# Down product of a gated MLP: sums of activations before each chain of products, the b chain continued from a1, and the plain units moved forward

## The chip, the cores and the metric

One Trainium2 chip, one of its cores. The metric is the device time of one execution in microseconds, as the median of several runs.

## What is computed

The kernel computes one layer of a decoder trunk on 512 tokens of 1024 channels in float32: three token mixers behind one input projection, their merge, and a gated MLP. The part around the change is the MLP, with D_FF = 3072:

```python
h = rms_norm(x, norm_ffn)
up = causal_dwconv(h @ w_up, ffn_conv_w, ffn_conv_b)      # 512 x 6144
a, b = up[..., :3072], up[..., 3072:]
x = x + (gelu(a) * b) @ w_down                            # 3072 -> 1024
out = rms_norm(x, final_norm)
```

## The kernel before

**Products.** Every float32 product is made of three products on TensorE: each operand is split into a high part (`split` L97, a copy on ScalarE that rounds) and a low part (L98, a subtraction on VectorE), and `mm3` (L104) adds high times high, high times low and low times high into one bank of PSUM. A product can start when the split of its operands is done.

**Up product.** The 3072 channels are 24 tiles of 128. A plain up unit makes one half of a tile (half 0 goes through the gelu, half 1 is the factor): 24 products, then the evacuation `up_evac` with the convolution (a scaled copy on ScalarE L1169, two scalar_tensor_tensor on VectorE L1171). With its second half a tile is finished by `up_mix`: the gelu on ScalarE L1183, the product on VectorE L1184. Tiles 0 to 19 are kept as float32 (`whole`); tiles 20 to 23 are split at once into a high and a low part (`halves`), which only the last stage of the kernel reads (`down_units`).

**Down product.** The first 20 tiles go through a scheme of seven products of half-size blocks instead of eight (`down_fast`, built by `seven`, L282 on). It has five groups p (four tiles each) and seven keys, a1, a2, c1, c2, b1, b2, b3; one key of one group is a fast unit of 12 products of 128x512. All five groups of one key follow each other and add up in the same two banks of PSUM; a2 goes on in a1's banks, c2 in c1's, b2 and b3 in b1's. After the last group of a key its two banks are read (`read`): VectorE adds them into the residual (`put`, L1335). a1's result is needed in several places; two copies on ScalarE (L1341) keep it, and three puts for each bank follow. Which activations a key multiplies: a1, a2 and b3 take quarters of the tiles as they are, c1, c2, b1 and b2 take sums of them. `sums(p)` makes six tensor_tensors of 128x256 for a group (L1311 to L1313), `sum4(p)` two more (L1321). `act_ready` then splits the quarter or sum. The weights of a1, c1, b1 and b3 stand in one buffer for each group, B11, into which GpSimd's accumulating transfers (`add`, L299) add the next matrix; those of b2 in B12 in the same manner; B21 and B22 are loaded directly.

**What sets the order.** Each unit carries steps with a lead: a step with lead 3 is issued three units ahead of the unit's products. `us` holds the seven plain units left at that point, u0 to u6: the second half of tile 20, then both halves of tiles 21, 22 and 23. `blend(us, down_fast(...))` puts five fast units behind each of them: u0 and a1, u1 and a2, u2 and c1, u3 and c2, u4 and b1, u5 and b2, u6 and b3. A planner turns this program into one stream for each engine; an engine runs its stream in order and stands still at the first instruction whose inputs, or whose buffer, are not ready. Buffers for activations, their splits, loaded weights and the evacuated halves all come from one pool `apool` of 51 slots; the splits of weights have four buffers each.

Of the kernel before, what the change touches and what calls it, by code (L numbers as in the profile page):

```python
# [13 lines left out]
AF = mybir.ActivationFunctionType  # L14
ALU = mybir.AluOpType
# [3 lines left out]
P = 128  # L19
# [20 lines left out]
AHEAD = 2  # L40
BRANCHES = (2, 0, 1)
NRAW = 3
HT = S // 2
# [14 lines left out]
def trunk(ctx: ExitStack, tc: tile.TileContext, x, xT, mem, memT, par, wdecay, wch, wv, wg, wmk,  # L58
          wmv, wrg, wbr, wout, wup, wdown, wdown2, gffn, gfin, out):
    nc = tc.nc  # L60
# [11 lines left out]
    def nm(s):  # L72
        uid[0] += 1
        return f"{s}_{uid[0]}"

    def fslot(shape=(P, S)):
        return apool.tile(list(shape), F32, tag="s", name=nm("f"))
# [7 lines left out]
    def bank(shape=(P, S)):  # L85
        return psm.tile(list(shape), F32, tag="mm", name=nm("mm"))

    def sbank(shape=(P, S)):
        return pss.tile(list(shape), F32, tag="sm", name=nm("sm"))
# [5 lines left out]
    def split(hi, lo, src, eng=None):  # L95

        nc.scalar.activation(hi, src, AF.Copy)  # L97
        return (eng or nc.vector).tensor_tensor(out=lo, in0=src, in1=hi.bitcast(F32), op=ALU.subtract)  # L98
# [45 lines left out]
    def made_unit(pre, fn):  # L144

        prog.append(("unit", pre, fn))
# [62 lines left out]
    ps = sbank((P, P))  # L209
# [72 lines left out]

    def seven(src, n, np, lhs, pre, read, far=AHEAD):

        raw, w, banks = {}, {}, {}

        def load(q, p):
            raw[q, p] = [fslot((P, n)) for _ in range(2)]
            for j in range(2):
                loads.append(nc.sync.dma_start(raw[q, p][j], src(q, p)[:, j, :]))

        def add(to, q, p):

            for j in range(2):
                nc.gpsimd.dma_start(raw[to, p][j], src(q, p)[:, j, :], accum_op=ALU.add)  # L299

        def direct(q, p):
            raw[q, p] = wpool.tile([P, 2, n], F32, tag="raw", name=nm("raw"), bufs=NRAW)
            loads.append(nc.sync.dma_start(raw[q, p], src(q, p)))

        def ready(key, q, p):
            hi = wpool.tile([P, 2, n], F32R, tag="whi", name=nm("whi"))
            lo = wpool.tile([P, 2, n], F32R, tag="wlo", name=nm("wlo"))
            if isinstance(raw[q, p], list):
                for j in range(2):
                    split(hi[:, j, :], lo[:, j, :], raw[q, p][j])  # L310
            else:
                split(hi, lo, raw.pop((q, p)))
            w[key, p] = hi, lo

        def run(key, p):
            ws = w.pop((key, p))
            b = key[0]
            for i in range(2):
                if key[1] == "1" and p == 0:
                    banks[b, i] = bank((P, n))  # L320
                mm3(banks[b, i], [(*lhs(key, p, j, i), ws[0][:, j, :], ws[1][:, j, :]) for j in range(2)],
                    key[1] == "1" and p == 0, p == np - 1, key[1] != "1")
                if p == np - 1:
                    read(key, i, banks[b, i])

        steps = {
            "a1": ("B11", [(6, lambda p: load("B11", p))]),
            "a2": ("B21", [(far, lambda p: direct("B21", p))]),
            "c1": ("B11", [(6, lambda p: add("B11", "B12", p))]),
            "c2": ("B22", [(far, lambda p: direct("B22", p))]),  # L330
            "b1": ("B11", [(6, lambda p: add("B11", "B22", p))]),
            "b2": ("B12", [(10, lambda p: load("B12", p)), (7, lambda p: add("B12", "B22", p))]),
            "b3": ("B11", [(6, lambda p: add("B11", "B21", p))]),
        }
        us = []
        for key, (q, before) in steps.items():
            for p in range(np):
                us.append(([(m, lambda f=f, p=p: f(p)) for m, f in before] +
                           [(AHEAD, lambda key=key, q=q, p=p: ready(key, q, p))] +
                           [(m, lambda f=f, p=p: f(p)) for m, f in pre.get(key, ())],  # L340
                           lambda key=key, p=p: run(key, p)))
        return us

    def run(*parts):

        for p in parts:
            if isinstance(p, tuple):
                unit(*p)
            else:
                for v in p:  # L350
                    made_unit(*v) if isinstance(v, tuple) else step(v)

    def blend(us, fast, steps=()):

        for i, u in enumerate(us):
            unit(*u)
            for l, f in ((fast, lambda v: made_unit(*v)), (steps, step)):
                for v in l[len(l) * i // len(us):len(l) * (i + 1) // len(us)]:
                    f(v)
# [407 lines left out]
    b2 = [u for d in range(KD) for u in branch(2, oc, d)]  # L767
# [173 lines left out]
    at = lambda a, i: by_chunk(a)[:, :, i:i + 1].broadcast_to([DK, NT, P])  # L941
# [350 lines left out]

    kept = {}

    def down_fast(at, np, acts, first, last):

        a_in, a_sp = {}, {}

        def sums(p):

            A = {}
            for j in range(2):
                ev, od = acts(2 * (2 * p + j)), acts(2 * (2 * p + j) + 1)
                for r in range(2):
                    A[1 + r, 1, j], A[1 + r, 2, j] = ev[:, r * HT:(r + 1) * HT], od[:, r * HT:(r + 1) * HT]
            s1, s2 = fslot((P, 2, HT)), fslot((P, 2, HT))
            tt = nc.vector.tensor_tensor
            for j in range(2):  # L1310
                tt(out=s1[:, j, :], in0=A[2, 1, j], in1=A[2, 2, j], op=ALU.subtract)  # L1311
                tt(out=s2[:, j, :], in0=s1[:, j, :], in1=A[1, 1, j], op=ALU.subtract)
                tt(out=A[2, 1, j], in0=A[1, 1, j], in1=A[2, 1, j], op=ALU.subtract)  # L1313
            both = lambda r, c: [A[r, c, j] for j in range(2)]
            a_in.update({("a1", p): both(1, 1), ("a2", p): both(1, 2), ("c1", p): s1, ("b1", p): s2,
                         ("b2", p): both(2, 1), ("b3", p): both(2, 2)})

        def sum4(p):
            a_in["c2", p] = a_in["a1", p]
            for j in range(2):  # L1320
                nc.vector.tensor_tensor(out=a_in["a1", p][j], in0=a_in["a2", p][j], in1=a_in["b1", p][:, j, :],  # L1321
                                        op=ALU.add)

        def act_ready(key, p):
            hi, lo = rslot((P, 2, HT)), rslot((P, 2, HT))
            a = a_in[key, p]
            if isinstance(a, list):
                for j in range(2):
                    split(hi[:, j, :], lo[:, j, :], a[j])
            else:  # L1330
                split(hi, lo, a)
            a_sp[key, p] = hi, lo

        def put(t, c, src, op=ALU.add):
            nc.vector.tensor_tensor(out=x2[t][c], in0=x2[t][c], in1=src, op=op)  # L1335

        def read(key, i, ps):
            if key == "a1":
                if first:
                    kept[i] = fslot()  # L1340
                    nc.scalar.activation(kept[i], ps, AF.Copy)  # L1341
                else:
                    nc.vector.tensor_tensor(out=kept[i], in0=kept[i], in1=ps, op=ALU.add)
                if not last:
                    return
                f = kept[i]
                put(2 + i, 0, f)
                put(i, 1, f, ALU.subtract)
                put(2 + i, 1, f, ALU.subtract)
            else:  # L1350
                put(*{"a2": (i, 0, ps), "c1": (2 + i, 1, ps), "c2": (i, 1, ps), "b1": (i, 1, ps, ALU.subtract),
                      "b2": (2 + i, 1, ps, ALU.subtract), "b3": (2 + i, 0, ps)}[key])

        pre = {k: [(2, lambda p, k=k: act_ready(k, p))] for k in ("a2", "c1", "b1", "b2", "b3")}
        pre["a1"] = [(3, sums), (1, lambda p: act_ready("a1", p))]
        pre["c2"] = [(3, sum4), (2, lambda p: act_ready("c2", p))]
        return seven(lambda q, p: wdown[at + p, int(q[1]) - 1, int(q[2]) - 1], HB, np,
                     lambda key, p, j, i: tuple(a[:, j, i * P:(i + 1) * P] for a in a_sp[key, p]), pre, read)

    def final_left(t):  # L1360

# [35 lines left out]
    acts = {}  # L1397
# [8 lines left out]
    us = up_units((0, 1, 2), whole, 3)  # L1406
# [4 lines left out]
    us = up_units((5, 8, 11, 14, 17, 19), whole) + up_units(range(20, NF), halves)  # L1411
    ahead = None
    for i in (3, 4, 6, 7, 9, 10, 12, 13, 15, 16, 18):
        f = up_fast(i, whole)
# [3 lines left out]
            run([lambda k=k, p=p: h2_ready(k, p) for k in ("b1", "b2") for p in range(2)])  # L1418
        ahead = f
    run([ahead["b1"]], us.pop(0), [ahead["b2"]], us.pop(0), [ahead["b3"]])  # L1420
    blend(us, down_fast(0, 5, lambda k: acts[k], True, True))
    step(lambda: gain_rows(gfin))
    weave(down_units(wdown2, lambda k: acts[20 + k], final, None, final_left, 2), [])

# [92 lines left out]
```

## Time and profile before

| | us |
|---|---|
| median of 3 runs (lowest, highest) | 927.07 (925.5, 930.22) |
| profiled execution: time | 926.82 |
| its span, first to last instruction | 925.1 |
| TensorE busy (98% of the span) | 909.3 |
| VectorE busy (72%) | 664.7 |
| ScalarE busy (58%) | 538.1 |
| GpSimd busy (16%) | 145.3 |

The span is what the profile shows of the execution. A product's busy time overlaps that of the next, so the step from the start of one to the start of the next tells more than the mean of one. What an engine waited for is named with the instruction that released it.

### The profile page before, as it was taken

To read this page: it belongs to the slowest core of one execution; us is meant where nothing else is said; L and a number is where in the kernel's file an instruction comes from. 1 tells how busy PE (TensorE), PEld (TensorE's weight loads), DVE (VectorE), ACT (ScalarE), POOL (GpSimd) and SP (SyncE) were. 2 spreads that over 40 slices of the span, in tenths; PEclk is the share of its full clock that TensorE was granted. 3 is DMA by queue.
4 is the path that set the end of the run, shared out by engine and by line. 5 is a ranking of instruction groups with operands and counts; after the bars stand their busy time and mean duration, and the time that the engine had idled before them with its cause. 6 is when DMAs were issued, how large, how long until landed. Compare 5 with 4: busy or idle time off the path is not lost.

```text
span 925.1 us, 13276 instructions
## 1 busy us (share of the span) xinstructions
PE 909.3 (98%) x4786; PEld 789.6 (85%) x4786; DVE 664.7 (72%) x1194; ACT 538.1 (58%) x933; POOL 145.3 (16%) x188
## 2 busy tenths in 40 slices
PE   9999999999999999999999999999999998999996
PEld 7899888888889998888888798999999986888885
DVE  6997755665688567747776678767776789877665
ACT  7775655585855468474534445656565555565544
POOL 0010000000233430330000000221221221306102
PEclk9999999999999999999999999999999999999999
DMA  7446223313468783321157324667676665779712
GB/s 246 143 134 214 91 88 101 88 46 116 115 162 180 176 207 119 114 86 52 52 165 250 114 58 109 180 145 185 158 178 164 150 158 126 162 199 228 167 41 91
DMA packets 55506, 128.55 MB, mean 139 GB/s; under 512 B 6625, under 2 KB 14481, under 8 KB 55441
## 3 DMA queue, kind: packets, MB, share of 16 engines
q1 hardware_dynamic: 37088, 94.99, 31.4%
q0 software_dynamic: 18208, 32.46, 20.4%
q8 instruction: 37, 0.61, 0.3%
q10 hardware_dynamic: 144, 0.26, 0.1%
q14 instruction: 29, 0.23, 0.1%
HBM read 123.23 MB, written 3.67 MB: 137 GB/s over the span
## 4 chain that ended last, share of the span: by engine, by line
PE 88%; DVE 5%; DMA 3%; ACT 2%; issue 1%; SPq 0%; POOL 0%; DVEq 0%; ACTq 0%; POOLq 0%
PE mm L104 76%; PE sm L104 7%; DMA f<-in_wv 2%; PE mm L436 2%; DVE wlo L98 1%; DVE f L1171 1%; DVE r L98 1%; ACT whi L97 1%; DMA raw<-in_wup 0%; ACT r L97 0%; PE sm L996 0%; PE sm L983 0%; PE sm L1010 0%; DMA raw<-in_wch 0%; DVE f L810 0%
## 5 line engine op out<-in xcount | busy, mean ns | idle before, releaser
L98 DVE TENSOR_TENSOR wlo<-raw,whi 128x1024 fp32r<-128x1024 f32 (+3 forms) x132 | 145.1, 1105 | 80.5 <-ACT whi L97 43.7
L97 ACT ACTIVATE whi<-raw 128x1024 fp32r<-128x1024 f32 (+3 forms) x132 | 125.0, 953 | 117.7 <-PE mm L104 89.0
L104 PE MATMUL mm<-whi,r 128*128 128x512 f32 (+2 forms) x568 | 169.6, 375 | 4.6 <-ACT r L97 4.6
L104 PEld LDWEIGHTS mm<-whi,r 128*128 128x128 f32 x568 | 106.1, 189 | 20.9 <-ACT r L97 5.3
L97 ACT ACTIVATE r<-f 128x512 fp32r<-128x512 f32 (+3 forms) x179 | 91.0, 551 | 41.4 <-DMA f<-in_wup 34.4
L104 PE MATMUL mm<-hh,whi 128*128 128x512 f32 x288 | 113.4, 394 | 0.0
L104 PE MATMUL mm<-hl,whi 128*128 128x512 f32 x288 | 112.7, 391 | 0.0
L104 PE MATMUL mm<-wlo,r 128*128 128x512 f32 (+2 forms) x284 | 106.4, 375 | 0.5 <-DVE wlo L98 0.5
L98 DVE TENSOR_TENSOR r<-f,r 128x512 fp32r<-128x512 f32 (+3 forms) x179 | 100.8, 598 | 6.6 <-ACT r L97 6.2
L104 PE MATMUL mm<-r,whi 128*128 128x512 f32 (+1 forms) x432 | 94.2, 367 | 0.0
L104 PEld LDWEIGHTS mm<-r,whi 128*128 128x128 f32 x432 | 75.2, 189 | 13.1
L1256 POOL DMA_DIRECT2D f<-in_wup x44 | 38.5, 989 | 285.4 <-PE sm L1147 131.2
L104 PE MATMUL mm<-r,r 128*128 128x256 f32 (+2 forms) x456 | 81.9, 329 | 0.0
L97 ACT ACTIVATE whi<-f 128x512 fp32r<-128x512 f32 (+2 forms) x90 | 48.1, 579 | 57.1 <-PE mm L104 44.1
L104 PEld LDWEIGHTS mm<-r,r 128*128 128x128 f32 (+1 forms) x456 | 68.7, 187 | 10.3 <-ACT r L97 0.7
L98 DVE TENSOR_TENSOR wlo<-f,whi 128x512 fp32r<-128x512 f32 (+2 forms) x90 | 53.7, 631 | 29.5 <-ACT whi L97 26.5
L104 PE MATMUL mm<-h2l,whi 128*128 128x512 f32 x184 | 71.8, 390 | 0.0
L104 PE MATMUL mm<-h2h,whi 128*128 128x512 f32 x184 | 71.6, 390 | 0.0
L104 PE MATMUL mm<-hh,wlo 128*128 128x512 f32 x288 | 71.5, 390 | 0.0
L104 PEld LDWEIGHTS mm<-hh,wlo 128*128 128x128 f32 x288 | 54.0, 188 | 11.2
L104 PEld LDWEIGHTS mm<-hh,whi 128*128 128x128 f32 x288 | 54.1, 188 | 10.9
L104 PEld LDWEIGHTS mm<-hl,whi 128*128 128x128 f32 x288 | 54.1, 188 | 10.7
(260 smaller groups left out, 1628.7 us busy)
## 6 DMA issues: line engine op xcount, KB each, us to landing
raw<-in_wch SPq DMA_DIRECT2D x39, 512.0 KB, 3.4
raw<-in_wup SPq DMA_DIRECT2D x26, 512.0 KB, 4.5
f<-in_wup SPq DMA_DIRECT2D x44, 256.0 KB, 5.9
f<-in_wup POOLq DMA_DIRECT2D x44, 256.0 KB, 5.4
f<-in_wdown POOLq DMA_DIRECT2D x40, 256.0 KB, 6.1
raw<-in_wbr SPq DMA_DIRECT2D x24, 384.0 KB, 3.1
raw<-in_wdown SPq DMA_DIRECT2D x14, 512.0 KB, 4.5
f<-in_wdown SPq DMA_DIRECT2D x20, 256.0 KB, 4.8
```

Source lines behind the costliest of these rows:

```text
L97: nc.scalar.activation(hi, src, AF.Copy)
L98: return (eng or nc.vector).tensor_tensor(out=lo, in0=src, in1=hi.bitcast(F32), op=ALU.subtract)
L104: nc.tensor.matmul(ps, lhsT=l, rhs=r, start=first and i == 0, stop=last and i == len(seq) - 1, skip_group_check=more)
L436: nc.tensor.matmul(ps[u], lhsT=w(a, u, k), rhs=xs["r"][k][j], start=k == 0 and i < n, stop=k == KD - 1 and i >= len(seq) - n)
L1171: nc.vector.scalar_tensor_tensor(out=a[:, j:], in0=ps[:, :S - j], scalar=col(C_FCW + 48 * (2 - j) + f), in1=a[:, j:], op0=ALU.mult, op1=AL ...
L1256: nc.gpsimd.dma_start(raw[q], src(more), accum_op=ALU.add)
```

## The change

- The b chain goes on in a1's banks, so that b1 adds to a1's sum without a reading between; a2 starts banks of its own, as c1 does. a1's banks are still read after a1's last group, but by one put for each bank; the copies and the other puts are gone.
- `sums` is taken apart: `parts` only names the quarters, `sum1` is made ahead of a2, `sum2` ahead of c1, `sum4` ahead of c2 and `sum3` ahead of b2, all with leads of 4 to 10 units. a1's split has lead 2 instead of 1.
- Instead of five fast units behind each plain unit there are 3, 2, 3, 2, 5, 5 and 15: u0 a1[0 to 2], u1 a1[3, 4], u2 a2[0 to 2], u3 a2[3, 4], u4 c1, u5 c2, u6 and then b1, b2, b3 without a plain unit.

```diff
-    def seven(src, n, np, lhs, pre, read, far=AHEAD):
+    def seven(src, n, np, lhs, pre, read, far=AHEAD, chained=False):
...
-            b = key[0]
+            b = "b" if chained and key == "a1" else key[0]
+            new = key in (("a1", "a2", "c1") if chained else ("a1", "b1", "c1"))
             for i in range(2):
-                if key[1] == "1" and p == 0:
+                if new and p == 0:
                     banks[b, i] = bank((P, n))
...
-            s1, s2 = fslot((P, 2, HT)), fslot((P, 2, HT))
-            tt = nc.vector.tensor_tensor
             for j in range(2):
-                tt(out=s1[:, j, :], in0=A[2, 1, j], in1=A[2, 2, j], op=ALU.subtract)
-                tt(out=s2[:, j, :], in0=s1[:, j, :], in1=A[1, 1, j], op=ALU.subtract)
-                tt(out=A[2, 1, j], in0=A[1, 1, j], in1=A[2, 1, j], op=ALU.subtract)
...
+        def sum1(p):
+            s1 = a_in["c1", p] = fslot((P, 2, HT))
+            tt(s1, a_in[21, p], a_in["b3", p], sub)
+
+        def sum2(p):
+            s2 = a_in["b1", p] = fslot((P, 2, HT))
+            tt(s2, a_in["c1", p], a_in["a1", p], sub)
...
+        def sum3(p):
+            s3 = a_in["b2", p] = a_in[21, p]
+            tt(s3, a_in["a1", p], s3, sub)
...
-                if first:
-                    kept[i] = fslot()
-                    nc.scalar.activation(kept[i], ps, AF.Copy)
...
-                put(2 + i, 0, f)
-                put(i, 1, f, ALU.subtract)
-                put(2 + i, 1, f, ALU.subtract)
...
-        pre["a1"] = [(3, sums), (1, lambda p: act_ready("a1", p))]
-        pre["c2"] = [(3, sum4), (2, lambda p: act_ready("c2", p))]
+        pre = {k: [(2, lambda p, k=k: act_ready(k, p))] for k in ("a1", "a2", "c1", "c2", "b1", "b2", "b3")}
+
+        pre["a1"].append((3, parts))
+        pre["a2"].append((np - 1, sum1))
+        pre["c1"].append((np - 1, sum2))
+        pre["c2"].append((np, sum4))
+        pre["b2"].append((2 * np, sum3))
...
-    blend(us, down_fast(0, 5, lambda k: acts[k], True, True))
+    down, n = down_fast(0, 5, lambda k: acts[k]), 0
+    for m, u in zip((3, 2, 3, 2, 5, 5, 15), us):
+        run(u, down[n:n + m])
+        n += m
```

The order of the instructions shows three places. The first is **ScalarE where a1 begins**. L1169 before and L1171 in the change are the evacuation of u0; `r_1466<-f_1449` before and `r_1462<-f_1445` in the change are the split of tile 20 into halves; `r_1468` before and `r_1456` in the change are the split for a1[1].

```order
L1169 ACTIVATE f_1465_7636<-mm_1464_7611,prm_76 128x512
L97 ACTIVATE whi_1484_7718<-f_1454_7564 128x512
L97 ACTIVATE whi_1484_7718<-f_1455_7565 128x512
L97 ACTIVATE r_1466_7642<-f_1449_7546 128x512
L97 ACTIVATE r_1468_7646<-f_1185_5944 128x256
L97 ACTIVATE r_1468_7646<-f_1215_6127 128x256
L97 ACTIVATE r_1476_7680<-f_1173_5865 128x256
L97 ACTIVATE r_1476_7680<-f_1305_6672 128x256
```

In the change the same stretch of ScalarE reads:

```order
L97 ACTIVATE r_1456_7583<-f_1185_5944 128x256
L97 ACTIVATE r_1456_7583<-f_1215_6127 128x256
L1185 ACTIVATE f_1445_7534<-f_1445_7534 128x512
L97 ACTIVATE whi_1471_7656<-raw_1470_7654 128x1024
L1185 ACTIVATE f_1452_7567<-f_1452_7567 128x512
L1171 ACTIVATE f_1461_7618<-mm_1460_7593,prm_76 128x512
L97 ACTIVATE whi_1473_7672<-f_1450_7550 128x512
L97 ACTIVATE whi_1473_7672<-f_1451_7551 128x512
L97 ACTIVATE r_1462_7624<-f_1445_7534 128x512
L97 ACTIVATE r_1466_7634<-f_1173_5865 128x256
L97 ACTIVATE r_1466_7634<-f_1305_6672 128x256
```

The split for a1[1] stood behind the split of tile 20; now it stands ahead of it, and ahead of u0's evacuation. The split for a1[2] (`r_1476` before, `r_1466` in the change) stands behind it in both.

The second is **VectorE up to the product that finishes tile 20** (L1184 before, L1186 in the change, on `f_1449` and `f_1445`).

```order
L1184 TENSOR_TENSOR f_1456_7581<-f_1456_7581,f_1457_7585 128x512
L1311 TENSOR_TENSOR f_1462_7603<-f_1173_5865,f_1275_6491 128x256
L1311 TENSOR_TENSOR f_1462_7603<-f_1305_6672,f_1233_6229 128x256
L1312 TENSOR_TENSOR f_1463_7604<-f_1462_7603,f_1173_5865 128x256
L1313 TENSOR_TENSOR f_1173_5865<-f_1173_5865 128x256
L1312 TENSOR_TENSOR f_1463_7604<-f_1462_7603,f_1305_6672 128x256
L1313 TENSOR_TENSOR f_1305_6672<-f_1305_6672 128x256
L1171 SCALAR_TENSOR_TENSOR f_1465_7636<-mm_1464_7611,prm_76,f_1465_7636 128x511
L98 TENSOR_TENSOR wlo_1471_7653<-f_1440_7487,whi_1470_7652 128x512
L1171 SCALAR_TENSOR_TENSOR f_1465_7636<-mm_1464_7611,prm_76,f_1465_7636 128x510
L98 TENSOR_TENSOR wlo_1479_7687<-f_1446_7517,whi_1478_7686 128x512
L1184 TENSOR_TENSOR f_1449_7546<-f_1449_7546,f_1465_7636 128x512
```

In the change the same stretch of VectorE reads:

```order
L1186 TENSOR_TENSOR f_1452_7567<-f_1452_7567,f_1453_7571 128x512
L98 TENSOR_TENSOR wlo_1472_7657<-raw_1470_7654,whi_1471_7656 128x1024
L1173 SCALAR_TENSOR_TENSOR f_1461_7618<-mm_1460_7593,prm_76,f_1461_7618 128x511
L1173 SCALAR_TENSOR_TENSOR f_1461_7618<-mm_1460_7593,prm_76,f_1461_7618 128x510
L98 TENSOR_TENSOR wlo_1474_7673<-f_1450_7550,whi_1473_7672 128x512
L1186 TENSOR_TENSOR f_1445_7534<-f_1445_7534,f_1461_7618 128x512
L98 TENSOR_TENSOR wlo_1474_7673<-f_1451_7551,whi_1473_7672 128x512
L98 TENSOR_TENSOR r_1463_7625<-f_1445_7534,r_1462_7624 128x512
```

The sums of L1311 to L1313, six for each group of a1, are no longer among the adds of the evacuation.

The third is **ScalarE at a plain unit ahead of the b chain**: before, the evacuation of u4 (L1169 on `mm_1598`), the split of its tile into halves (`r_1600`) and that for b1[2] (`r_1604`); in the change the split for b1[1] (`r_1608`), the evacuation of u6 (L1171 on `mm_1612`), the split of its tile into halves (`r_1614`) and that for b1[2] (`r_1618`).

```order
L97 ACTIVATE whi_1610_8384<-f_1446_7517 128x512
L97 ACTIVATE whi_1610_8384<-f_1447_7518 128x512
L1169 ACTIVATE f_1599_8344<-mm_1598_8319,prm_76 128x512
L97 ACTIVATE whi_1614_8408<-f_1454_7564 128x512
L97 ACTIVATE whi_1614_8408<-f_1455_7565 128x512
L97 ACTIVATE r_1600_8350<-f_1563_8159 128x512
L97 ACTIVATE r_1604_8360<-f_1463_7604 128x512
```

In the change, at u6, ScalarE's stream reads:

```order
L97 ACTIVATE r_1608_8383<-f_1531_7967 128x512
L97 ACTIVATE whi_1624_8478<-f_1458_7589 128x512
L97 ACTIVATE whi_1624_8478<-f_1459_7590 128x512
L1171 ACTIVATE f_1613_8420<-mm_1612_8395,prm_76 128x512
L97 ACTIVATE whi_1628_8502<-f_1586_8267 128x512
L97 ACTIVATE whi_1628_8502<-f_1587_8268 128x512
L97 ACTIVATE r_1614_8426<-f_1575_8223 128x512
L97 ACTIVATE r_1618_8436<-f_1536_7994 128x512
L97 ACTIVATE r_1622_8460<-f_1541_8023 128x512
```

The evacuation now stands behind b1[1]'s split and a further split of weights, with the split for b1[2] behind both as before. In the built program the evacuation of u6 waits for the last product of b1[1], and the split for b1[1] for one of the last products of b1[0]; before, the evacuation of u4 waited for u4's own last product.

## Rows read from the trace of the kernel before

**Rows 1.** The page: the span, and busy time of the engines.

```profile
span 925.1 us, 13276 instructions
...
PE 909.3 (98%) x4786; PEld 789.6 (85%) x4786; DVE 664.7 (72%) x1194; ACT 538.1 (58%) x933; POOL 145.3 (16%) x188
```

**Rows 2.** TensorE's waits: engine, line, releaser; us in total, times, longest.

```profile
PE mm L104 <- ACT r L97: 4.6, 1, 4.6
```

**Rows 3.** The chain that ended last: its last link (start, us).

```profile
769.05 148.81 PE mm L104 x648
```

**Rows 4.** TensorE's timeline around a1 and where u4 meets b1: start, us, instruction.

```profile
763.87 0.61 PE L104 MATMUL mm<-whi,r 128*128 128x512 f32 x2
769.05 0.50 PE L104 MATMUL mm<-whi,r 128*128 128x512 f32 x1 [4.57 <-ACT r L97]
...
774.18 0.39 PE L104 MATMUL mm<-wlo,r 128*128 128x512 f32 x1
...
842.42 1.98 PE L104 MATMUL mm<-h2h,wlo 128*128 128x512 f32 x8
844.23 0.39 PE L104 MATMUL mm<-whi,r 128*128 128x512 f32 x1
```

**Rows 5.** Stretches: us, busy PE, PEld, DVE, ACT, POOL, granted clock, DMA share, GB/s.

```profile
769.00:774.00 5.00, 4.95 (x15) 3.84 (x16) 5.00 (x15) 1.84 (x6) 1.75 (x2) 0.66 0.95 163
774.00:780.00 6.00, 6.00 (x28) 4.98 (x27) 6.00 (x13) 3.90 (x7) 0.86 (x1) 1.00 0.41 67
```

**Rows 6.** ScalarE's timeline around a1.

```profile
764.52 1.15 ACT L97 ACTIVATE whi<-f 128x512 fp32r<-128x512 f32 x2 [1.94 <-PE mm L104]
768.06 2.47 ACT L97 ACTIVATE r<-f 128x512 fp32r<-128x512 f32 x7 [2.39 <-DVE f L1184]
...
780.51 0.60 ACT L1341 ACTIVATE f<-mm 128x512 f32<-128x512 f32 x1 [0.30 <-PE mm L104]
```

**Rows 7.** VectorE's timeline: the product that finishes tile 20.

```profile
767.35 0.68 DVE L1184 TENSOR_TENSOR f<-f,f 128x512 f32<-128x512 f32 x1
```

**Rows 8.** VectorE's groups from 750 to 769: count, busy us, mean ns.

```profile
L1312 DVE TENSOR_TENSOR f<-f,f 128x256 f32<-128x256 f32 x6 | 2.5, 418 | 0.0
L1313 DVE TENSOR_TENSOR f<-f 128x256 f32<-128x256 f32 x6 | 2.5, 418 | 0.0
L1311 DVE TENSOR_TENSOR f<-f,f 128x256 f32<-128x256 f32 x6 | 2.3, 418 | 0.0
```

**Rows 9.** Groups from 760 to 918: ScalarE's splits of 128x512.

```profile
L97 ACT ACTIVATE r<-f 128x512 fp32r<-128x512 f32 x14 | 8.4, 622 | 5.4 <-DVE f L1184 2.4 <-PE mm L104 2.3 <-DVE r L98 0.7
```

**Rows 10.** ScalarE's and VectorE's timeline behind u4.

```profile
844.43 0.78 ACT L1169 ACTIVATE f<-mm,prm 128x512 f32<-128x512 f32 x1 [0.66 <-PE mm L104]
...
845.70 1.53 DVE L1171 SCALAR_TENSOR_TENSOR f<-mm,prm,f 128x511 f32<-128x511 f32 x2
...
847.26 0.69 DVE L1184 TENSOR_TENSOR f<-f,f 128x512 f32<-128x512 f32 x1
...
848.21 1.14 ACT L97 ACTIVATE r<-f 128x512 fp32r<-128x512 f32 x2
```

**Rows 11.** DMA queues and issues from 825 to 866 (KB each, median us to landing).

```profile
q0 software_dynamic: 2456, 4.48, 60.3%
q1 hardware_dynamic: 2053, 4.81, 35.1%
...
f<-in_wdown POOLq DMA_DIRECT2D x20, 256.0 KB, 11.8
```

**Rows 12.** GpSimd's and ScalarE's timeline ahead of b2[4].

```profile
858.85 0.87 POOL L299 DMA_DIRECT2D f<-in_wdown  x1 [1.24 <-DMA f<-in_wdown]
861.12 0.86 POOL L299 DMA_DIRECT2D f<-in_wdown  x1 [1.41 <-issue]
...
869.84 0.63 ACT L97 ACTIVATE whi<-f 128x512 fp32r<-128x512 f32 x1 [4.34 <-DMA f<-in_wdown]
871.02 0.63 ACT L97 ACTIVATE whi<-f 128x512 fp32r<-128x512 f32 x1 [0.55 <-DMA f<-in_wdown]
```

More of the change, by code (lines that the diff above doesn't have):

```diff
@@ L316, in run @@
             ws = w.pop((key, p))
-            b = key[0]
+            b = "b" if chained and key == "a1" else key[0]
+            new = key in (("a1", "a2", "c1") if chained else ("a1", "b1", "c1"))
             for i in range(2):
-                if key[1] == "1" and p == 0:
+                if new and p == 0:
                     banks[b, i] = bank((P, n))
                 mm3(banks[b, i], [(*lhs(key, p, j, i), ws[0][:, j, :], ws[1][:, j, :]) for j in range(2)],
-                    key[1] == "1" and p == 0, p == np - 1, key[1] != "1")
+                    new and p == 0, p == np - 1, not new)
                 if p == np - 1:
@@ L1291, in up_fast, with down_fast, parts @@
         return {key: (p, lambda key=key: run(key)) for key, p in pre.items()}
-    kept = {}
-    def down_fast(at, np, acts, first, last):
+    def down_fast(at, np, acts):
         a_in, a_sp = {}, {}
-        def sums(p):
+        sub, add = ALU.subtract, ALU.add
+        def parts(p):
             A = {}
@@ L1307, in sums, with tt @@
                     A[1 + r, 1, j], A[1 + r, 2, j] = ev[:, r * HT:(r + 1) * HT], od[:, r * HT:(r + 1) * HT]
-            s1, s2 = fslot((P, 2, HT)), fslot((P, 2, HT))
-            tt = nc.vector.tensor_tensor
+            both = lambda r, c: [A[r, c, j] for j in range(2)]
+            a_in.update({("a1", p): both(1, 1), ("a2", p): both(1, 2), (21, p): both(2, 1), ("b3", p): both(2, 2)})
+        def tt(out, a, b, op):
             for j in range(2):
-                tt(out=s1[:, j, :], in0=A[2, 1, j], in1=A[2, 2, j], op=ALU.subtract)
-                tt(out=s2[:, j, :], in0=s1[:, j, :], in1=A[1, 1, j], op=ALU.subtract)
-                tt(out=A[2, 1, j], in0=A[1, 1, j], in1=A[2, 1, j], op=ALU.subtract)
-            both = lambda r, c: [A[r, c, j] for j in range(2)]
-            a_in.update({("a1", p): both(1, 1), ("a2", p): both(1, 2), ("c1", p): s1, ("b1", p): s2,
-                         ("b2", p): both(2, 1), ("b3", p): both(2, 2)})
-        def sum4(p):
[L1319 to L1322, printed above, removed]
+                o, x, y = (v[j] if isinstance(v, list) else v[:, j, :] for v in (out, a, b))
+                nc.vector.tensor_tensor(out=o, in0=x, in1=y, op=op)
+        def sum1(p):
[4 more added lines that the diff above has]
+            tt(s2, a_in["c1", p], a_in["a1", p], sub)
+        def sum4(p):
+            s4 = a_in["c2", p] = a_in["a2", p]
+            tt(s4, s4, a_in["b1", p], add)
+        def sum3(p):
+            s3 = a_in["b2", p] = a_in[21, p]
+            tt(s3, a_in["a1", p], s3, sub)
         def act_ready(key, p):
@@ L1337, in read @@
         def read(key, i, ps):
-            if key == "a1":
-                if first:
-                    kept[i] = fslot()
-                    nc.scalar.activation(kept[i], ps, AF.Copy)
[L1342 to L1346, printed above, removed]
-                put(2 + i, 0, f)
-                put(i, 1, f, ALU.subtract)
-                put(2 + i, 1, f, ALU.subtract)
[L1350 to L1354, printed above, removed]
-        pre["a1"] = [(3, sums), (1, lambda p: act_ready("a1", p))]
-        pre["c2"] = [(3, sum4), (2, lambda p: act_ready("c2", p))]
+            put(*{"a1": (i, 0, ps), "a2": (i, 0, ps), "c1": (2 + i, 1, ps), "c2": (i, 1, ps), "b1": (i, 1, ps, sub),
+                  "b2": (2 + i, 1, ps, sub), "b3": (2 + i, 0, ps)}[key])
+        pre = {k: [(2, lambda p, k=k: act_ready(k, p))] for k in ("a1", "a2", "c1", "c2", "b1", "b2", "b3")}
[4 more added lines that the diff above has]
+        pre["b2"].append((2 * np, sum3))
         return seven(lambda q, p: wdown[at + p, int(q[1]) - 1, int(q[2]) - 1], HB, np,
-                     lambda key, p, j, i: tuple(a[:, j, i * P:(i + 1) * P] for a in a_sp[key, p]), pre, read)
+                     lambda key, p, j, i: tuple(a[:, j, i * P:(i + 1) * P] for a in a_sp[key, p]), pre, read, chained=True)
     def final_left(t):
```

## The prediction, made before the changed kernel ran

> **What bounds the kernel now.** Read first the page's head: TensorE is busy 909.3 of the span's 925.1 us [rows 1], so the time is the number of products times their step, plus the moments when TensorE stands still. Then TensorE's list of waits: one entry is of any size, 4.6 us, on a split that ScalarE makes (L97) [rows 2]. Then the chain that ended last: its last link is TensorE alone, from 769.05 for 148.81 us [rows 3]. The one large wait ends exactly where this link begins. Everything the change touches lies around that wait or inside that link, so a gain can only come from the wait, and a loss only from a hole torn into the link.
>
> The sum is made against the profiled execution: it took 926.82 us against a median of 927.07, 0.25 apart, so I add the sum to the median as it is. A difference under 0.5% (4.6 us) is about what a measurement of this kernel can't tell from none: faster begins at 922.4, slower at 931.7.
>
> **Part 1, removed: the wait at a1.** The products before it start last at 764.10 (the second of the two of the row at 763.87), the next at 769.05, and the step from one product to the next is 0.227 (eight from 842.42 to 844.23) [rows 4]. The hole is 769.05 - 764.10 - 0.23 = 4.72. Behind it TensorE is granted 0.66 of its clock in the stretch 769 to 774 and 1.00 in the next [rows 5], so it falls from its level of 2.4 GHz to 1.2 after standing still for these 4.7 us; the 15 products from 769.05 to 774.18 [rows 4] took 5.13 where 15 steps take 3.40, another 1.73. Together **6.45**.
>
> What made it: ScalarE ran the splits of weights at 764.52 and then stood until 768.06 for VectorE's product at L1184 [rows 6], which VectorE gave from 767.35 to 768.03 [rows 7]. That product finishes up tile 20; its split into halves is not needed until the very end, but it stands on ScalarE ahead of a1[1]'s split (first order fence). VectorE was late because 18 sums of activations (L1311 to L1313, 418 ns each [rows 8]) were pushed in between its evacuations, the sums of all three first groups at once (second fence).
>
> In the change ScalarE makes a1[1]'s split before the halves, and none of those sums is on VectorE there. The hole and its low clock go: **-6.45**. Left may be a short wait at a1[2], whose split still stands behind the halves; I count 0, the bound is 1: two splits of 128x512 at 622 ns [rows 9], less what overlaps.
>
> **Part 2, removed for nothing.** Two copies on ScalarE of 0.60 (L1341) [rows 6] and four puts on VectorE, each of the shape of the L1184 product (0.68 [rows 7]). Neither engine is behind anywhere in the link, whose only cover for them is TensorE's unbroken run [rows 3]; they count 0. Products, loads and accumulating transfers are as many as before.
>
> **Part 3, moved: the sums at c1.** sum1 now runs before a2, sum2 before c1, sum4 before c2, sum3 before b2, so VectorE's work is spread; at c1[2] two of them stand ahead of the product that finishes a plain tile. Two of 418 ns, with 0.34 from one start to the next, make 0.67 late, and the slack at such a place in the link before was about 0.3 to 0.4 (below): **+0.25**, bounds 0 and 0.7.
>
> **Part 4, new: the wait at b1[2].** Before, a plain unit (24 products, 5.44 us) stood ahead of every five fast units (12 products, 2.72 us each). Now the last plain unit u6 is followed by 15 fast ones, b1, b2 and b3, and two more tiles have been split into halves by then. In the pool of 51 slots 42 are then held for good (20 activations, ten loads of B11, five sums, six halves, one gate tile, against four halves before); nine are left for ten loads of B12 and the splits under way. The built program shows what this does: the split of b1[1] waits for the last products of b1[0], and the evacuation of u6 on ScalarE waits, not for u6's own last product, but for the last of b1[1], whose slots it takes. And it stands on ScalarE ahead of b1[2]'s split (third fence).
>
> The first costs a little: the split (0.62), one hand-over on each side (0.05 each) and the product's own 0.39 make 1.1, against three steps, 0.68, until b1[1] is due: **+0.42**.
>
> The second is the old hole again. Its pattern is in the trace before, behind u4: evacuation on ScalarE at 844.43, the two adds of L1171 at 845.70, the product at 847.26, two splits at 848.21 that end at 849.35 [rows 10]: 4.92 from the evacuation's start to the split that b1[2] needs. There it cost nothing, as the evacuation started when u4 ended (844.23 is b1[0]'s first product [rows 4]) and b1[0] and b1[1], 5.44 us of products, covered it with 0.3 to spare. In the change both of these have run before the evacuation may start, so nothing covers it. It starts 0.2 after b1[2] is due (the last product's 0.39 and the hand-over, less a step). In the order of the change the two adds and the splits of weights alternate on VectorE: 0.78 + 3.2 + 0.05 + 0.55 + 0.62 + 0.1 for hand-overs = 5.3, a little over the 4.92. So the hole is 0.2 + 5.3 = **+5.5**, with the bounds 5.1 (the row of before) and 6. Behind it the clock should fall as in [rows 5]: **+1.7**, bounds 0 (it doesn't fall) and 3 (all of the next 5 us at half speed, and a little more).
>
> **Part 5, moved: the accumulating transfers.** Without a plain unit the last five groups want their weights sooner after each other. POOL's accumulating loads took a median of 11.8 us to land between 825 and 866, with 60.3% of the DMA engines' time [rows 11]. The last two, issued at 858.85 and 861.12, held ScalarE at 869.84 for 4.34 and at 871.02 [rows 12], about two microseconds before TensorE wanted b2[4]. The 20 accumulating and 14 other transfers of that stretch filled 95% of the DMA engines for its 41 us (60.3 and 35.1%); in the change the same work, begun near 831 without pause, would be through by 872 to 875. The new hole delays the use of b2[4]'s weights to about 878.2 by itself: **0**. Without the hole they would be due at 872.3, and 0 to 2 us would be lost there.
>
> **Sum.** -6.45 + 0.25 + 0.42 + 5.5 + 1.7 = **+1.4**, so 927.07 + 1.4 = **928.5**. The hole is moved from 764 to about 858, not removed.
>
> **The rivals.**
> A, faster: the wait at b1[2] does not arise, because the evacuation is released earlier than I read. Then only -6.45 + 0.25 + 0.42 stand, 921.3, perhaps a microsecond more for b2[4]'s weights. For it: the hole at a1 is surely measured, and that before had no wait for a slot. Against it: the built order names b1[1]'s last product. Chance 0.11.
> B, slower: the last accumulations land late. The place is b2[4]; it decides if they land after 878.2, more than 19 us behind their issue near 859. The median of 11.8 [rows 11] speaks against it, but the DMA engines are nearly full there, and the issues may be held up behind the same full pool. Price: the 4.34 of [rows 12] uncovered and another 1.7 of clock, 934.5. Chance 0.13. The Trainium skill (SBUF — State Buffer, the box on VectorE blocking DMA) names another way to a late landing: a transfer issued by GpSimd waits for its descriptors while VectorE runs an operation in a mode that takes both ports; the time would again be B's. By the same page's section Who interferes with whom a tensor_tensor has no such mode, and no row here shows a landing that waits for VectorE.
> C, the change does only part of what it says: a1[2]'s split, behind the halves of tile 20, still waits. 929.5; chance 0.06.
> D, the clock does not fall behind the new hole: 926.8; chance 0.08.
> The forecast itself: 0.62.
>
> **How the numbers follow.** Forecast, C and D lie within 0.5%: 0.76. A is faster: 0.11. B is slower: 0.13. The range takes in the forecast with its bounds, C and D: 928.5 - 0.25 - 0.4 - 1.7 - 0.3 and a spread of runs of about 1.5 give 924 below; 928.5 + 1.3 + 0.5 + 0.5 + 1 and the near half of B give 933 above. Left out are A and the far half of B, under 0.2.
>
> **What would show it.** In TensorE's waits of the changed kernel the 4.6 us entry is gone between a1[0] and a1[1], and one of 5 to 6 us on a split at L97 stands between 854 and 860, with b1[1] and b1[2] on either side; the granted clock in the 5 us behind it is 0.6 to 0.7; ScalarE's evacuation of u6 starts after b1[1]'s last product; the last link of the chain ends about 919. I am wrong if no wait over 2 us stands there (A), if a wait of TensorE for b2[4]'s weights does (B), or if the wait at a1 is still there.

## The result and the profile after

The change made the kernel a little slower: median 929.5 us (927.31 to 932.88, 20 runs) against 926.97 (925.21 to 930.22, 20 runs) before, ratio 1.0029 with the 95% interval 1.0019 to 1.0039. That is 2.5 to 2.7 us, inside the 0.5% that was called "the same"; the forecast was 928.5.

The profiled execution took 928.11 us, 1.4 under the median. TensorE's busy time and the span, from the page of the changed kernel (busy us, share, instructions), answer to [rows 1]:

```profile
span 926.3 us, 13280 instructions
...
PE 910.2 (98%) x4786; PEld 789.3 (85%) x4786; DVE 662.3 (72%) x1190; ACT 537.1 (58%) x931; POOL 145.6 (16%) x188
```

TensorE's waits (us in total, times, longest) answer to [rows 2]. One large wait of 4.6 has become one of 5.4 and a small one:

```profile
PE mm L104 <- ACT r L97: 5.7, 2, 5.4
```

TensorE's timeline (start, us, instruction, idle time before it and who ended it) shows where they are. 760.36 is a1[0]'s first product, 766.26 is a1[2]'s; 851.27 and 859.66 are the first products of b1[1] and b1[2], and the last one is the eighth step behind that:

```profile
760.36 0.39 PE L104 MATMUL mm<-whi,r 128*128 128x512 f32 x1
...
766.26 0.50 PE L104 MATMUL mm<-whi,r 128*128 128x512 f32 x1
...
850.34 0.61 PE L104 MATMUL mm<-whi,r 128*128 128x512 f32 x2
851.27 0.50 PE L104 MATMUL mm<-whi,r 128*128 128x512 f32 x1 [0.32 <-ACT r L97]
...
853.69 0.61 PE L104 MATMUL mm<-whi,r 128*128 128x512 f32 x2
859.66 0.80 PE L104 MATMUL mm<-whi,r 128*128 128x512 f32 x1 [5.35 <-ACT r L97]
...
863.11 0.40 PE L104 MATMUL mm<-whi,r 128*128 128x512 f32 x1
```

Nothing stands still around 764 any more. The hole at b1[2] is 859.66 - 853.92 (the second product of the row at 853.69) - 0.23 = 5.51; that at b1[1] is 851.27 - 850.57 - 0.23 = 0.47. The stretches of all engines (length; busy PE, PEld, DVE, ACT, POOL; granted clock; DMA share; GB/s) answer to [rows 5]:

```profile
854.00:859.50 5.50, 0.30 (x2) 0.00 (x0) 3.59 (x6) 2.86 (x5) 2.95 (x5) 1.00 1.11 247
859.50:864.50 5.00, 4.84 (x15) 3.87 (x16) 1.66 (x3) 1.01 (x3) 2.33 (x3) 0.66 1.14 208
864.50:870.00 5.50, 5.50 (x25) 4.41 (x24) 5.14 (x12) 4.71 (x12) 0.00 (x0) 1.00 1.12 202
```

The clock falls behind the hole just as it did at a1: the eight steps from 859.66 to 863.11 took 3.45 instead of 1.81, 1.64 lost. ScalarE's timeline shows the cause, and VectorE's the link in the middle; they answer to [rows 10]:

```profile
850.58 0.63 ACT L97 ACTIVATE r<-f 128x512 fp32r<-128x512 f32 x1 [2.98 <-issue]
...
854.34 0.78 ACT L1171 ACTIVATE f<-mm,prm 128x512 f32<-128x512 f32 x1 [2.08 <-PE mm L104]
855.02 1.14 ACT L97 ACTIVATE whi<-f 128x512 fp32r<-128x512 f32 x2
858.45 1.15 ACT L97 ACTIVATE r<-f 128x512 fp32r<-128x512 f32 x2 [2.30 <-DVE f L1186]
```

```profile
855.15 0.75 DVE L1173 SCALAR_TENSOR_TENSOR f<-mm,prm,f 128x511 f32<-128x511 f32 x1 [2.01 <-ACT f L1171]
...
857.68 0.68 DVE L1186 TENSOR_TENSOR f<-f,f 128x512 f32<-128x512 f32 x1
```

u6's last product started near 847.8, but its evacuation at 854.34, when b1[1] was through; from there it is 5.3 us to b1[2] (859.66), against the 4.92 of [rows 10] up to the split's end.

The chain that ended last needs care here. Where it comes past the hole it names a transfer:

```profile
847.95 7.88 DMA f<-in_wdown
855.83 0.14 DVE wlo L98
...
858.45 1.16 ACT r L97 x2
859.66 5.44 PE mm L104 x16
```

A reader of this alone would say that late weights made the hole. VectorE was busy with L1173 until 855.90, so the split at 855.83 did not in fact come late for a transfer. Nor did anything else in that stretch: in the rows of both engines above, from 854.34 to 859.66, every idle time was ended by TensorE, ScalarE or VectorE, none by a transfer.

From a1[0]'s first product to the end of the last is the part that the change touches. In the profile of before it began at 761.60:

```profile
761.60 0.39 PE L104 MATMUL mm<-whi,r 128*128 128x512 f32 x1
```

and ended at 769.05 + 148.81 = 917.86 [rows 3]: 156.26. After it runs from 760.36 to 883.36 + 35.66:

```profile
883.36 35.66 PE mm L104 x156
```

158.66, 2.40 more. This is close to the difference of the medians; what came before a1 took 1.2 us less in the one profiled execution, most likely by chance, and so the spans differ by only 1.2.

### The profile page after: what moved, and what is told of

Read it like the earlier page. It is cut to its first block, busy times and chain, and to the rows that moved or that the text cites. A ratio compares the mean times of both kernels' runs of the same rounds, so it can differ in the third digit from the quotient of the medians.

```text
span 926.3 us, 13280 instructions
## 1 busy us (share of the span) xinstructions
PE 910.2 (98%) x4786; PEld 789.3 (85%) x4786; DVE 662.3 (72%) x1190; ACT 537.1 (58%) x931; POOL 145.6 (16%) x188
## 4 chain that ended last, share of the span: by engine, by line
PE 92%; DMA 2%; DVE 2%; ACT 2%; issue 1%; SPq 0%; ACTq 0%; POOLq 0%
PE mm L104 80%; PE sm L104 7%; PE mm L438 2%; DMA f<-in_wdown 2%; DVE wlo L98 1%; DMA raw<-in_wup 0%; PE sm L998 0%; PE sm L985 0%; ACT whi L97 0%; PE sm L1012 0%; DMA raw<-in_wch 0%; PE sm L1149 0%; ACT r L97 0%; PE sm L603 0%; PE sm L1041 0%
```

## The experiments

Eight kernels were run. Two questions stood behind them: what makes the new hole (the slots, the sums and the chain, or late weights), and what made the old one (the sums on VectorE, or the order of the splits on ScalarE). Each ratio is against the unchanged kernel run beside it: its median was 926.02 us beside the even order, 53 slots, the order alone and u6 between b1 and b2, and 927.01 us beside the other four.

### One plain unit ahead of every five fast ones again

```diff
-    for m, u in zip((3, 2, 3, 2, 5, 5, 15), us):
+    for m, u in zip((5, 5, 5, 5, 5, 5, 5), us):
```

> The changed kernel with the plain units put back to one ahead of every five fast units (5, 5, 5, 5, 5, 5, 5); the spread sums and the chain from a1 into b stay. Theory: the new hole comes from the order of the units (u6's evacuation waits for slots that b1[1] holds, ahead of b1[2]'s split on ScalarE). Then no wait of TensorE over 1 us is left after a1[0], the sums alone have taken away the old hole, and the time is 927.0 - 6.5 + 0.5 = 921.0 (920 to 922.5; ratio to the kernel before about 0.9935). Rival one, the chain or the later sums make the hole: a wait of some 5 us on a split stays at b1[2], 929 to 930. Rival two, late weights: the transfers have the same leads counted in units but more time, so a wait for a transfer would shrink, not vanish; 923 to 926.

920.46 us (918.87 to 921.76), ratio 0.9935 (0.9921 to 0.9949). No wait of TensorE of over 0.15 us is left from a1 on; the last link of the chain runs without a break for 105 us:

```profile
806.07 105.33 PE mm L104 x463
```

The spread sums, a1's earlier split and the chain together take the old hole away at no cost; the new hole belongs to the order of the units. This version beats both kernels.

### 53 slots instead of 51

```diff
-NSLOT = 51
+NSLOT = 53
```

> The changed kernel with 53 slots in the pool of activations instead of 51. In its built program u6's evacuation waits for b1[0]'s last product instead of b1[1]'s, and b1[1]'s split waits for nothing of b1[0]; a split of weights behind the evacuation still waits for b1[1]'s last product, as one of four weight buffers comes free there. Theory: the 0.48 wait at b1[1] goes; the 5.5 wait at b1[2] shrinks to what stands behind that split of weights: 0.2 late + two splits of weights 1.14 + two splits of activations 1.14 = 2.5, and the low clock behind it by 0 to 1.6; time 929.5 - 0.5 - 3.0 - 0.8 = 925.2 (924 to 926.5). Rival, the slots are not the cause (late weights): the wait stays at 5 to 6 us, 929 to 930.

925.5 us (925.0 to 931.25), ratio 0.9993 (0.9975 to 1.001), as expected. The wait at b1[1] is gone, that at b1[2] is 857.61 - 854.59 - 0.23 = 2.79 where 2.5 was worked out:

```profile
854.36 0.61 PE L104 MATMUL mm<-whi,r 128*128 128x512 f32 x2
857.61 0.55 PE L104 MATMUL mm<-whi,r 128*128 128x512 f32 x1 [2.64 <-ACT r L97]
```

ScalarE's timeline: the evacuation runs 2.7 us (one fast unit) earlier in relation to the products, and the next thing that waits for b1[1] is the pair of weight splits at 855.01, behind which b1[2]'s split (the second of 856.41) stands:

```profile
852.29 0.78 ACT L1171 ACTIVATE f<-mm,prm 128x512 f32<-128x512 f32 x1 [3.38 <-PE mm L104]
852.97 1.15 ACT L97 ACTIVATE whi<-f 128x512 fp32r<-128x512 f32 x2
855.01 1.15 ACT L97 ACTIVATE whi<-f 128x512 fp32r<-128x512 f32 x2 [0.90 <-PE mm L104]
856.41 1.78 ACT L97 ACTIVATE r<-f 128x512 fp32r<-128x512 f32 x3 [0.25 <-DVE f L1186]
```

So the slots made the first half of the hole: it shrank by 5.51 - 2.79 = 2.72, just what the evacuation moved. By the built order a weight buffer that comes free late would have made the second half anyway; no run with more weight buffers tested that. Two more slots can also let transfers start earlier, so this run alone would not clear the late weights; that no idle time of ScalarE or VectorE in the hole was ended by a transfer does, whatever the chain named. Behind 2.8 us of standing still the clock falls too:

```profile
857.00:861.50 4.50, 3.89 (x10) 3.08 (x11) 3.02 (x5) 2.54 (x6) 2.63 (x3) 0.62 1.13 210
```

### The order of the units alone

```diff
-    blend(us, down_fast(0, 5, lambda k: acts[k], True, True))
+    down, n = down_fast(0, 5, lambda k: acts[k], True, True), 0
+    for m, u in zip((3, 2, 3, 2, 5, 5, 15), us):
+        run(u, down[n:n + m])
+        n += m
```

> The kernel before with only the plain units moved (3, 2, 3, 2, 5, 5, 15); sums all ahead of a1, a1 copied out as before. In its built program u6's evacuation waits for b1[1]'s last product just as in the changed kernel, and u1 stands ahead of a1[1]. Theory: the hole at b1[2] is there, 5.5 + 0.5 + 1.6 of clock, and at a1 u1's products cover nearly all of the old hole (0.5 left): 927.0 - 6.5 + 0.5 + 7.6 + 0.4 = 929.0 (927.5 to 930.5). So the order alone would give about the time of the whole change. Rival, the chain or the later sums make the new hole: no wait over 2 us at b1[2], 921 to 922 if u1 covers the old hole, 927 if it doesn't.

931.55 us (930.43 to 932.96), ratio 1.0056 (1.004 to 1.0071). The new hole is there to the hundredth, 862.10 - 856.36 - 0.23 = 5.51, and 0.47 at b1[1], with neither the chain nor the spread sums:

```profile
853.71 0.50 PE L104 MATMUL mm<-whi,r 128*128 128x512 f32 x1 [0.32 <-ACT r L97]
...
856.13 0.61 PE L104 MATMUL mm<-whi,r 128*128 128x512 f32 x2
862.10 0.79 PE L104 MATMUL mm<-whi,r 128*128 128x512 f32 x1 [5.35 <-ACT r L97]
```

The old hole shrinks to a wait of 0.30, as u1's products stand in it. The time is 2.5 above what was worked out, though. With all sums still ahead of a1, products start late by 0.9 in all near 796; the steps up to these two are 0.49 and 0.57 instead of 0.23:

```profile
796.00 0.50 PE L104 MATMUL mm<-whi,r 128*128 128x512 f32 x1
...
797.37 1.08 PE L104 MATMUL mm<-whi,r 128*128 128x512 f32 x3 [0.18 <-DVE r L98]
```

The low clock behind the new hole cost 1.9 and not 1.6: the nine steps from 862.10 to 866.05 took 3.95 instead of 2.04.

```profile
862.70 0.63 PE L104 MATMUL mm<-wlo,r 128*128 128x512 f32 x1
...
865.68 0.54 PE L104 MATMUL mm<-whi,r 128*128 128x512 f32 x1
```

In the profiled execution another 0.9 lies behind TensorE's last product, in the closing transfer, most likely by chance.

### u6 between b1 and b2

```diff
-    for m, u in zip((3, 2, 3, 2, 5, 5, 15), us):
+    for m, u in zip((3, 2, 3, 2, 5, 10, 10), us):
```

> The changed kernel with u6 moved from ahead of b1 to between b1 and b2 (3, 2, 3, 2, 5, 10, 10). In its built program u6's evacuation waits only for u6's own last product and stands ahead of no split that b1 needs. Theory: neither wait at b1[1] nor at b1[2]; 929.5 - 0.6 - 5.5 - 1.6 = 921.8 (920.5 to 923). Rival, late weights: with b1 earlier than its plain unit the accumulating loads for b1 are due 5.4 us sooner, and a wait for a transfer or for a split of weights of several us shows among b1's units: 925 to 930.

930.79 us (930.52 to 932.11), ratio 1.0051 (1.0037 to 1.0066): the expectation was wrong, and its rival right in kind, though not in the place (it looked among b1's units) and 0.8 over its range. The waits at b1[1] and b1[2] are gone, but a new one of 876.28 - 868.03 - 0.23 = 8.02 stands in front of b2[2] (the split that released it is the first of the row at 875.31 below):

```profile
867.80 0.61 PE L104 MATMUL mm<-whi,r 128*128 128x512 f32 x2
876.28 0.79 PE L104 MATMUL mm<-whi,r 128*128 128x512 f32 x1 [7.86 <-ACT r L97]
```

On ScalarE, b2[2]'s split stands behind splits of weights that wait for accumulating loads; the last of these was issued at 864.30 and landed 10.5 us later:

```profile
862.60 0.63 ACT L97 ACTIVATE whi<-f 128x512 fp32r<-128x512 f32 x1 [5.91 <-DMA f<-in_wdown]
...
874.77 0.63 ACT L97 ACTIVATE whi<-f 128x512 fp32r<-128x512 f32 x1 [1.03 <-DMA f<-in_wdown]
875.31 1.84 ACT L97 ACTIVATE r<-f 128x512 fp32r<-128x512 f32 x5
```

The queues from 831 to 875 fill the DMA engines to 98%:

```profile
q0 software_dynamic: 2880, 5.24, 66.6%
q1 hardware_dynamic: 2016, 4.46, 31.2%
```

This is what the prediction's rival B feared, at b2[2] instead of b2[4], in an order without the hole at b1[2] that gave the transfers 7.6 us.

### The same with 53 slots

```diff
-NSLOT = 51
+NSLOT = 53
```

> The kernel of the fourth experiment (u6 between b1 and b2), which lost 8.2 us at b2[2] to accumulating loads that landed late, with 53 slots instead of 51. The loads of B12 that these transfers add to wait for slots; with two more each is released one fast unit (2.7 us) sooner. Theory, the full pool holds up the transfers: the wait falls to 3 to 5.5, time 930.8 - 3 to 5 = 927 (925.5 to 928). Rival, the DMA engines' own rate (they are busy 98% there): the wait stays at 7 to 8.5, 930 to 931.5.

929.76 us (928.06 to 930.59), ratio 1.0023 (1.0007 to 1.0039). TensorE's wait at b2[2] is 5.9 instead of 7.9, between the two expectations:

```profile
873.77 0.79 PE L104 MATMUL mm<-whi,r 128*128 128x512 f32 x1 [5.92 <-ACT r L97]
```

The full pool accounts for some 2 of the 8 us. Less than half of that came back as time: behind this hole twelve steps of 0.43 us follow, up to 879.48, against six behind that of 8.0 us, and from a1[0]'s first product to the end of TensorE's last it is 159.7 us instead of 160.5. The engines stay 98% full (68.2 and 30.2% of the two queues from 831 to 875), so their rate is the likely reason for the other 6; that was not shown by a run that lightens them.

### One number: a1's split two units ahead

```diff
-        pre["a1"] = [(3, sums), (1, lambda p: act_ready("a1", p))]
+        pre["a1"] = [(3, sums), (2, lambda p: act_ready("a1", p))]
```

> The kernel before with one number changed: a1's split is issued two units ahead instead of one. The sums stay in front of the product that finishes tile 20, and a1[2]'s split still stands behind the halves of tile 20, but a1[1]'s now stands ahead of them. Theory: two things made the old hole, the order of the splits and the sums on VectorE. Here a1[1] starts on time and a1[2], due at 767.05 in the time of the profile before, waits for the halves split at 768.1 + 0.6 and its own 0.4: a hole of 2.0 instead of 4.72, with 0 to 1.6 of low clock; 927.0 - 6.5 + 2.0 + 0.8 = 923.3 (922 to 925). Rival one, the order of the splits alone made it: no wait over 0.5 us, 920.5 to 921.5. Rival two, the sums alone made it: the wait stays near 4.7, 926 to 927.

922.47 us (920.87 to 924.32), ratio 0.9948 (0.9931 to 0.9966). The time is as expected, the way to it only in part. a1[1] starts on time, and VectorE still finishes tile 20 only at 768.07. But the planner moved 15 of u1's products in front of a1[2], so not a1[2] waits, but these, 1.15 us, for their own weights:

```profile
766.46 0.50 PE L104 MATMUL mm<-h2h,whi 128*128 128x512 f32 x1 [1.15 <-ACT whi L97]
```

Nothing falls behind it in the clock. This run doesn't separate the two causes cleanly, since u1's products cover what a1[2] would have waited.

### The sums without the lead

```diff
-        pre = {k: [(2, lambda p, k=k: act_ready(k, p))] for k in ("a1", "a2", "c1", "c2", "b1", "b2", "b3")}
+        pre = {k: [(1 if k == "a1" else 2, lambda p, k=k: act_ready(k, p))] for k in ("a1", "a2", "c1", "c2", "b1", "b2", "b3")}
```

in the kernel of the first experiment.

> The kernel of the first experiment (spread sums, chain, one plain unit ahead of every five fast ones) with a1's split issued one unit ahead, as before, instead of two. No sums stand in front of the product of tile 20, but a1[1]'s split is behind the halves of tile 20 again. Theory: the halves split then starts some 4.9 us after u0's last product ends (760.56 to 765.27 in the profile of the change), and with its 0.6 and a1[1]'s 0.75 behind it a1[1] can start 6.2 us behind a1[0]'s start, when it is due after 2.7: a hole of 3.5, with up to 1.6 of low clock; 920.5 + 3.5 + 1.2 = 925.2 (923.5 to 926). Rival, the sums alone made the old hole: no wait over 0.5 us, 920.5 to 921.5.

923.75 us (922.83 to 925.55), ratio 0.9961 (0.9946 to 0.9977). With no sums on VectorE, a1[1] still waits behind the halves of tile 20, 766.16 - 763.71 - 0.23 = 2.22:

```profile
763.48 0.61 PE L104 MATMUL mm<-whi,r 128*128 128x512 f32 x2
766.16 0.50 PE L104 MATMUL mm<-whi,r 128*128 128x512 f32 x1 [2.06 <-ACT r L97]
```

The expectation of 3.5 was too much: the halves started at 765.19, right behind ScalarE's weight splits, and VectorE's product was no longer what they waited for. The clock holds behind this hole:

```profile
766.00:771.00 5.00, 4.84 (x21) 3.79 (x21) 5.00 (x15) 3.87 (x11) 1.59 (x2) 1.00 0.97 145
```

The old hole of 4.7 has two causes: with the sums moved and the order kept, 2.2 remain. Moving the sums first takes off 2.5 and the low clock, the order of the splits the rest. These are shares in that sequence and not two prices that add up: the earlier split alone saved 4.5 us (922.47 against 927.01), the moved sums without it 3.3, and both together, with the chain, 5.6 (920.46 against 926.02).

### Without the chain from a1 into b

```diff
-            put(*{"a1": (i, 0, ps), "a2": (i, 0, ps), "c1": (2 + i, 1, ps), "c2": (i, 1, ps), "b1": (i, 1, ps, sub),
+            if key == "a1":
+                f = fslot()
+                nc.scalar.activation(f, ps, AF.Copy)
+                put(2 + i, 0, f)
+                put(i, 1, f, ALU.subtract)
+                put(2 + i, 1, f, ALU.subtract)
+                return
+            put(*{"a2": (i, 0, ps), "c1": (2 + i, 1, ps), "c2": (i, 1, ps), "b1": (i, 1, ps, sub),
...
-                     lambda key, p, j, i: tuple(a[:, j, i * P:(i + 1) * P] for a in a_sp[key, p]), pre, read, chained=True)
+                     lambda key, p, j, i: tuple(a[:, j, i * P:(i + 1) * P] for a in a_sp[key, p]), pre, read)
```

in the kernel of the first experiment.

> The kernel of the first experiment without the chain from a1 into b: a1's banks go on with a2, a1's sum is copied by ScalarE and put three times by VectorE for each bank, as before. Sums and leads as in the change. Theory: the chain itself is worth nothing, as TensorE's unbroken run covers the copies and puts: 920.5 (919.5 to 921.5), and no wait over 0.6 us behind a1[0]. Rival, the copies and puts cost something where a1 ends (0.60 for a copy and 2.0 for three puts on each bank ahead of other work on VectorE): a wait of 1 to 2 us where a2 begins or two units later, 921.5 to 922.5.

920.68 us (919.01 to 922.13), ratio 0.9925 (0.99 to 0.9951), the same as with the chain: from a1[0]'s first product to the end of TensorE's last it is 150.3 us in both profiles. The copies and puts cost nothing where TensorE has work, as Part 2 said.

## Why the prediction was right

- **Part 1** (-6.45): right. The hole and its low clock are gone from 764; at a1[2] about 0.16 is left, 0.11 at its first product (766.26) and slower steps behind. The mechanism was right as well, and both of its halves count: with the sums moved 2.2 us of the hole stayed, and the earlier split took these away.
- **Part 2** (0): right, by the run without the chain.
- **Part 3** (+0.25): 0.38 at c1[2], inside the bounds of 0 and 0.7.
- **Part 4**: the wait at b1[1] was put at 0.42 and is 0.47; the hole at b1[2] at 5.5 and is 5.51; the low clock behind it at 1.7 and is 1.64. That the last came so near is in part luck: the figure was taken over from the one hole of before, and behind the other holes of this case the low clock cost from nothing to 2.8 (last section). That the evacuation waits for slots and not for its product was read from the built order, and 53 slots moved it by one fast unit, as that reading says. The order alone gives the same hole.
- **Part 5** (0): right for the change. The other half of its statement, that without the hole 0 to 2 us would be lost to late weights, was not tried as such; with u6 moved into the b chain 8.0 were lost, so in a dense order the transfers are a bound of their own, and the size was too small for that order. The Trainium skill (SBUF — State Buffer, the box on VectorE blocking DMA) would look for such lateness in VectorE's operations; the rows here show DMA engines that are 98% full, and no run shows a landing that waited for VectorE.
- **The sum** came out at +2.4 to 2.5 instead of +1.4. The measured sizes above come to -6.45 + 0.16 + 0.38 + 0.47 + 5.51 + 1.64 = +1.7; most of the other 0.7 is small change that was counted at nothing. Where one key follows another in the same banks without a plain unit between them, the first product waits for VectorE's reading of the bank. At the end of b2 the three products from 882.72 take 1.10 us where three take 0.84, with the put beside them:

```profile
881.36 0.84 PE L104 MATMUL mm<-whi,r 128*128 128x512 f32 x3
...
882.72 1.10 PE L104 MATMUL mm<-whi,r 128*128 128x512 f32 x3
```

```profile
882.53 0.68 DVE L1345 TENSOR_TENSOR m<-m,mm 128x512 f32<-128x512 f32 x1
```

That is 0.26, and 0.11 at the end of b1. With 53 slots the delay at the end of b1 is larger, and TensorE's list of waits names the put there:

```profile
PE mm L104 <- DVE m L1345: 0.2, 1, 0.2
```

In the even order, where a plain unit stands between these keys, no step there is slow. A further 0.11 at a2[2] and slow steps of 0.1 behind b1[1] are other delays, whose cause was not traced.

Of the rivals, A's time (921.3) is what the even order reached (920.5), but not by A's way: in the order of the change the evacuation was not released earlier. B came true in another order. D fell: the clock did fall. C left at most 0.2.

## What to carry to other kernels

A wait on an engine that runs its stream in order is removed only if nothing else in that stream waits in its place. Ask of every instruction that was moved what its buffer waits for, not only its inputs: here an evacuation that was ready at 848 ran at 854, because its slots were still held by a product that the new order had put ahead of it. Small fillers spread evenly did three things at once in this kernel: they covered the chains of other engines, they let buffers come free, and they gave transfers time. Packing them at one end gave up the first two at b1[2], and the third showed when u6 alone was moved into the b chain.

## What was not expected of the hardware

The granted clock stayed at 1.00 behind TensorE's hole of 2.2 us (the run with the sums alone), and fell to 0.62 to 0.66 in the stretch behind holes of 2.8, 4.7 and 5.5 us; the steps there are 0.43 us, the lower level of 1.2 GHz. The loss did not follow the hole's length: 1.7 us behind the hole of 2.8, 1.73 behind 4.7, 1.64 behind that of 5.5 in the change and 1.9 behind the equal one of the order alone, 2.8 behind 6.1 and 1.6 behind 8.0 (u6 between b1 and b2, with 53 slots and with 51). So the hole that 53 slots cut from 5.5 to 2.8 gave back only its own length, and the one that they cut from 8.0 to 6.1 not even that.

Accumulating loads took 10.6 to 11.9 us to land (medians from 831 to 875 in the change and in the run with u6 in the b chain) while the DMA engines were 97 to 98% full, and two more slots took 2 us off the wait for them.
